# A one-core decoder block: square-root seeds in the first and last norm, and a re-timed attention loop

## The chip, the cores and the metric

The kernel runs on one core of a Trainium2 chip. The metric is the device time of one execution in microseconds. Before the change, three runs took 1623.13 to 1624.22 us, with a median of 1623.73 us. One further execution was taken with the hardware profiler, and all views of the profile come from it. The engines are named as the profile names them: PE is the matrix engine (PEld its weight loads), DVE the vector engine, ACT the activation engine, POOL the general engine, SP the queue that issues most transfers. A `q` behind an engine's name means its sequencer.

## The reference

The program computes one layer of a decoder on 512 positions of width 1024, in float32:

```python
h = layer_norm(x, ln_in_g, ln_in_b)
mix = hybrid_mixer(h, ...)          # 16 SSD heads and 8 latent-attention heads, one output projection
h = layer_norm(DEEPNORM_ALPHA * h + mix, ln_mix_g, ln_mix_b)
ffn = peer(h, w_query, sub_keys, u_table, v_table)   # 8 heads, top 16 of 128 x 128 experts
h = layer_norm(DEEPNORM_ALPHA * h + ffn, ln_ffn_g, ln_ffn_b)

def layer_norm(x, g, b):
    mu = jnp.mean(x, -1, keepdims=True)
    var = jnp.mean(jnp.square(x - mu), -1, keepdims=True)
    return (x - mu) * lax.rsqrt(var + NORM_EPS) * g + b
```

The attention of one head is a causal softmax of scores (a part without and a part with rotary positions) times values, for four blocks of 128 queries. The SSD branch is a chunked state-space recurrence, gated with silu(z) and scaled by a root-mean-square norm; then both branches go through one output projection of 2048 x 1024.

## The kernel before

All instructions are written in one order by hand (`tc.manual_schedule()`); each engine and each queue runs its own in that order, and semaphores hold an instruction until what it reads is there and what it overwrites has been read. Every product is made of three (`mm3`, L72 to L74): weights and activations are each split into a high part in a shorter format and a low part, the remainder.

**Weights.** `Stream` (`win`) carries all weights. Per item there is a load (L91, on SP, into `wir`, three buffers), a high part by ACT (`his`, L109, into `wih`) and a low part by DVE (`splits`, L119, into `wil`). `get(n)` (through `item()`) first splits the items up to n + `la`, and a split issues the load of the item three further on. `la` is 2 before the attention.

**First norm** (L265 to L286). x lies in `XH` in four blocks of 128 positions and is worked in two pairs. For a pair, DVE makes the statistics (L268, L269), then the inverse root of the variance by `rsqrt` (L133 to L138: a seed from the exponent's bits and three Newton rounds), then `nm` (L274). ACT and DVE scale the blocks (L279, L281), and PE transposes them into eight PSUM banks (L284). Behind the first pair ACT makes the high parts of weights 0 and 1 (`win.his(2)`). Then, for each of eight slices, ACT and DVE write `ht`, `HH` and `HL` (L291 to L296), and PE starts the first two projections with them (L72 to L74).

**Attention** (the loop over `st` from 0 to 38, L832 on). Step `st` belongs to head `st // 4` and query block `st % 4`, and the stages of a head follow one another as a pipeline. In the order of the code a step holds: `p_scale` of the block two steps back (reciprocal of the sum on DVE, L783; scaling on ACT for the two longer blocks, L785, on DVE for the two shorter, L787); `p_tr` of six steps back (transposes of the weights, L796, whose high part ACT and whose low part DVE writes, `evac`, L695 and L696); `scores` (into PSUM, maximum on DVE, L769); `y_tr` in eight of the steps (`GST[3]` is 7, so steps 16 to 23: transposes of the SSD result, L541, read out by ACT and DVE, L547 and L548); one part of the projections of the next head (`q_pe` with L708 and L711, `qk_nope`, `v_proj`; each first part takes one item of weights); from step 28 one weight of the output projection for the fourth block of positions (`w_out_step`); `p_exp` (ACT, L777); in steps 8 to 15 one part of the SSD norm (`gate2`, L521 to L534); and `p_v`, the product with the values of seven steps back, whose result `MO` goes through `evac` into `MH` and `ML`. `p_tr`, `scores` and `y_tr` share one ring of four PSUM buffers (`pt`); the projections and the values of `v_proj` share two (`pu`). After the loop comes the tenth weight for the fourth block, and then the output projection for the other three blocks, with its own items.

**After that** come the second norm, the PEER stage (queries, top 16, and two long passes over the tables, with gathers for the fourth block), in which PE is busy nearly without a gap, and the last norm. `ln_out(b)` (L1504 to L1528) does it for blocks 0, 1 and 2 in turn: add the residual, statistics, the inverse root by `norm_chain` (L144 to L154, the same bit seed and three rounds), two scalings, and the transfer to the output. For block 2 the two first scalings (L1518) stand between the Newton operations.

## Time and profile before

| what | value |
|---|---|
| median of three runs | 1623.73 us (1623.13 to 1624.22) |
| profiled execution | 1623.08 us |
| its span, first to last instruction | 1621.3 us |
| PE / DVE / ACT / POOL busy | 1581.0 / 1357.4 / 708.1 / 481.4 us |
| mean granted clock of PE | 0.998 |
| HBM traffic | 360 MB read, 32 MB written |

The time holds the span and what the execution needs around it. Lines of the page's groups name the source line, engine, operation, and out<-in by the program's names; behind the bar stand busy time and the mean duration of one in ns. In the order of time a line begins with its start and its duration in us, and a bracket at its end tells how long the engine sat idle and what ended that. In PE's lines the durations of neighbours overlap, since products are pipelined; what counts is the distance of the starts.

### The profile page before, as it was taken

The page shows a single profiled execution, that of the slowest core. Times are in us where ns is not written, and L with a number is a line of the kernel's source. Part 1 is how long each engine was busy: PE and PEld are TensorE (multiplying, and loading weights), DVE is VectorE, ACT ScalarE, POOL GpSimd, SP SyncE. Part 2 cuts the span into 40 slices and gives each one's busy share as a digit, 9 for nine tenths or more (in the row PEclk, how much of TensorE's full clock was granted, in tenths as well). Part 3 has the DMA queues.
Part 4 walks back from the last instruction along what each step waited for, and adds up shares of the span by engine and source line. Part 5 has one row for each costly group of instructions (what it writes and reads, how often), then busy time and mean ns, then how long its engine had stood idle before and what let it go on. Part 6 is the DMA issues. An engine that isn't in the chain of part 4 may idle for free.

```text
span 1621.3 us, 23808 instructions
## 1 busy us (share of the span) xinstructions
PE 1581.0 (98%) x8643; PEld 1393.0 (86%) x8643; DVE 1357.4 (84%) x2564; ACT 708.1 (44%) x1231; POOL 481.4 (30%) x340
## 2 busy tenths in 40 slices
PE   6999999999999999999999999999999999999997
PEld 5777878888888999999999999999999999888886
DVE  8978667747799999998478888888888888889877
ACT  5575467641433445555433433333333333333341
POOL 0000010000133223100035555555555555555300
PEclk9999999999999999999999999999999999999999
DMA  6242122364432459767689999999999999999973
GB/s 243 94 157 91 46 77 57 114 235 143 133 92 81 136 179 344 272 241 255 201 282 360 358 341 342 359 352 343 349 351 350 343 343 360 353 338 362 334 226 118
DMA packets 152253, 395.42 MB, mean 244 GB/s; under 512 B 12776, under 2 KB 65720, under 8 KB 150344
## 3 DMA queue, kind: packets, MB, share of 16 engines
q1 hardware_dynamic: 108408, 238.35, 43.3%
q0 software_dynamic: 43584, 155.29, 26.1%
q8 instruction: 68, 1.11, 0.3%
q14 instruction: 49, 0.40, 0.1%
q10 hardware_dynamic: 144, 0.26, 0.0%
HBM read 359.99 MB, written 31.78 MB: 242 GB/s over the span
## 4 chain that ended last, share of the span: by engine, by line
PE 74%; DVE 18%; ACT 3%; issue 3%; DMA 2%; SPq 0%; DVEq 0%; ACTq 0%
PE va L1377 10%; PE va L1381 10%; PE va L1378 10%; PE pu L72 9%; PE pu L74 8%; PE pu L73 8%; PE pa L74 3%; PE pa L73 3%; PE pa L72 3%; DVE ij L1134 2%; DVE wil L119 2%; DVE t L955 1%; DMA wir<-ut 1%; DVE ti L959 1%; DVE ti L952 1%
## 5 line engine op out<-in xcount | busy, mean ns | idle before, releaser
L109 ACT ACTIVATE wih<-wir 128x1024 fp32r<-128x1024 f32 (+2 forms) x269 | 278.0, 1034 | 275.0 <-DMA wir<-v 94.4
L119 DVE TENSOR_TENSOR wil<-wir,wih 128x1024 fp32r<-128x1024 f32 (+1 forms) x254 | 301.9, 1189 | 98.7 <-ACT wih L109 53.8
L74 PE MATMUL pu<-XTH,wil 128*128 128x368 f32 x1008 | 331.8, 329 | 1.0 <-DVE wil L119 0.9
L72 PE MATMUL pu<-XTH,wih 128*128 128x368 f32 x904 | 299.0, 331 | 1.3 <-ACT act L1230 1.3
L73 PE MATMUL pu<-XTL,wih 128*128 128x368 f32 x904 | 296.9, 328 | 0.0
L1378 PE MATMUL va<-wil,Ph 128*128 128x512 f32 x726 | 282.7, 389 | 0.0
L1415 POOL DMA_INDIRECT row<-u,ix x128 | 190.9, 1491 | 256.7 <-DVE row L1426 126.1
L1415 POOL DMA_INDIRECT row<-v,ix x128 | 193.8, 1514 | 168.5 <-DVE ac L1432 142.9
L74 PEld LDWEIGHTS pu<-XTH,wil 128*128 128x128 f32 x1008 | 189.1, 188 | 1.7 <-DVE wil L119 1.6
L72 PEld LDWEIGHTS pu<-XTH,wih 128*128 128x128 f32 x904 | 169.5, 188 | 4.8 <-ACT act L1230 1.9
L73 PEld LDWEIGHTS pu<-XTL,wih 128*128 128x128 f32 x904 | 169.8, 188 | 2.9
L1377 PE MATMUL va<-wih,Ph 128*128 128x512 f32 x432 | 168.6, 390 | 0.0
L1432 DVE SCALAR_TENSOR_TENSOR ac<-row,hd,ac 128x1024 f32<-128x1024 f32 x128 | 164.0, 1281 | 3.5 <-DMA row<-v,ix 1.2
L1378 PEld LDWEIGHTS va<-wil,Ph 128*128 128x128 f32 x726 | 136.3, 188 | 25.8
L1230 ACT ACTIVATE act<-pu 128x368 f32<-128x368 f32 x126 | 59.9, 476 | 219.5 <-PE pu L74 219.4
L1426 DVE SCALAR_TENSOR_TENSOR row<-row,x 128x1024 f32<-128x1024 f32 x128 | 150.3, 1219 | 3.9 <-DMA row<-u,ix 3.7
L109 ACT ACTIVATE wihx<-wir 128x1024 fp32r<-128x1024 f32 x67 | 71.1, 1061 | 146.1 <-DMA wir<-v 120.5
L1381 PE MATMUL va<-wih,Pl 128*128 128x512 f32 x432 | 133.3, 390 | 0.0
L119 DVE TENSOR_TENSOR wil<-wir,wihx 128x1024 fp32r<-128x1024 f32 x62 | 75.8, 1223 | 51.4 <-issue 36.8
L1377 PE MATMUL va<-wihx,Ph 128*128 128x512 f32 x294 | 114.9, 391 | 0.0
L1381 PEld LDWEIGHTS va<-wih,Pl 128*128 128x128 f32 x432 | 81.0, 188 | 17.2
L1377 PEld LDWEIGHTS va<-wih,Ph 128*128 128x128 f32 x432 | 81.2, 188 | 15.9
(458 smaller groups left out, 3066.3 us busy)
## 6 DMA issues: line engine op xcount, KB each, us to landing
wir<-ut SPq DMA_DIRECT2D x128, 512.0 KB, 5.7
wir<-v SPq DMA_DIRECT2D x128, 512.0 KB, 6.6
gsp<-stg SPq DMA_DIRECT2D x12, 1920.0 KB, 7.4
gt<-gsp SPq DMA_DIRECT2D x30, 768.0 KB, 9.9
wir<-wo SPq DMA_DIRECT2D x26, 512.0 KB, 3.6
wir<-wf SPq DMA_DIRECT2D x18, 512.0 KB, 3.3
wir<-wqr SPq DMA_DIRECT2D x16, 512.0 KB, 3.6
de<-acd POOLq DMA_DIRECT2D x8, 512.0 KB, 5.2
```

The costliest lines, as they stand in the source:

```text
L72: T.matmul(ps, lh, rh, start=start, stop=False)
L73: T.matmul(ps, lh, rl, start=False, stop=False)
L74: T.matmul(ps, ll, rh, start=False, stop=stop)
L109: A.activation(h, r, AF.Copy)
L119: self.lo(n).tensor_tensor(l, r, h, op=OP.subtract)
L1230: A.activation(ACT[c][:, :NU], ps, AF.Gelu)
L1377: T.matmul(va[b][e], Ph[:, bs], h[:, cs], start=c == 0, stop=False)
L1378: T.matmul(va[b][e], Ph[:, bs], l[:, cs], start=False, stop=False)
L1381: T.matmul(va[b][e], Pl[:, bs], h[:, cs], start=False, stop=c == 127)
L1415: G.indirect_dma_start(out=R[s], out_offset=None, in_=I["u"] if s < 128 else I["v"], in_offset=bass.IndirectOffsetOnAxis(ap=ix[:, s % 128: ...
L1426: V.scalar_tensor_tensor(r, r, 1.0, x3, op0=OP.mult, op1=OP.mult, accum_out=hd[:, s:s + 1])
L1432: V.scalar_tensor_tensor(ac, r, hd[:, s - 128:s - 127], ac, op0=OP.mult, op1=OP.add)
```

## The change

It touches three places.

1. First norm: `sqrt_rs` takes the place of `rsqrt`. ACT computes the square root of variance plus eps; DVE takes the reciprocal as the seed and makes one Newton round (square, product, correction). A tile `eps` is added, and a root of ones early on ACT. The high part of weight 0 is made behind the second pair's root, ahead of its scaling, and that of weight 1 behind the second pair's transposes.
2. Attention: `la` is 1 up to step 25, 2 from step 26, 1 at step 36 and 2 after the loop. `y_tr` moves from steps 16 to 23 into steps 17 to 24. For the last head (h = 7) all four blocks are scaled on DVE.
3. Last norm: block 2 uses `sqrt_chain`, in which ACT makes the root and DVE the reciprocal and one round; the two first scalings of the block stand ahead of the reciprocal and ahead of the round. Ahead of the last products, ACT runs a `Square` and a `Sqrt` on one column.

```diff
+    def sqrt_rs(p, v, shape, tag, eps):
+        h, q, y, a = (p.tile(shape, F32, name=tag + n) for n in "hqya")
+        A.activation(q, v, AF.Sqrt, bias=eps)
+        V.tensor_scalar(h, v, EPS, -0.5, op0=OP.add, op1=OP.mult)
+        V.reciprocal(y, q)
+        V.tensor_tensor(a, y, y, op=OP.mult)
+        V.tensor_tensor(a, a, h, op=OP.mult)
+        V.scalar_tensor_tensor(y, a, 1.5, y, op0=OP.add, op1=OP.mult)
+        return y
+
+    def sqrt_chain(p, mv, tag, out, eps):
+        h, q, a, y = (p.tile([128, 1], F32, name=tag + n) for n in "hqay")
+        A.activation(q, mv[:, 1:2], AF.Sqrt, bias=eps)
+        V.tensor_scalar(h, mv[:, 1:2], EPS, -0.5, op0=OP.add, op1=OP.mult)
+        yield
+        V.reciprocal(y, q)
+        yield
+        V.scalar_tensor_tensor(a, y, h, y, op0=OP.mult, op1=OP.mult)
+        yield
+        V.scalar_tensor_tensor(y, a, 1.5, y, op0=OP.add, op1=OP.mult)
+        out.append(y)
+        yield
...
+    eps = lnp.tile([128, 1], F32, name="eps")
+    V.memset(eps, EPS)
+    w0 = lnp.tile([128, 1], F32, name="w0")
+    A.activation(w0, ones[:, 0:1], AF.Sqrt, bias=eps)
...
-        ve = lnp.tile([128, 2], F32, name="ve", bufs=2)
-        V.tensor_scalar(ve, mv4[:, bs, 1], EPS, None, op0=OP.add)
-        rs = rsqrt(lnp, ve, [128, 2], "l0")
+        rs = sqrt_rs(lnp, mv4[:, bs, 1], [128, 2], f"l{p}", eps)
         V.scalar_tensor_tensor(nm, mv4[:, bs, 0], -1.0, rs, op0=OP.mult, op1=OP.mult)
+        if p:
+            win.his(1)
...
-        if p == 0:
-            win.his(2)
+    win.his(2)
     win.splits(1)
...
-        if qb > 1:
+        if qb > 1 and h < 7:
             A.activation(P[:, :n], P[:, :n], AF.Copy, scale=sm)
...
+    win.la = 1
     for st in range(39):
         h, q = divmod(st, 4)
+        if st == 26:
+            win.la = 2
...
-        if GST[3] + 9 <= st < GST[3] + 17:
-            y_tr(st - GST[3] - 9)
+        if GST[3] + 10 <= st < GST[3] + 18:
+            y_tr(st - GST[3] - 10)
...
             if st < 37:
+                win.la = 1 if st == 36 else 2
                 w_out_step(acc3, (3,), st - 28)
...
+    win.la = 2
     w_out_step(acc3, (3,), 9)
...
-        ch = norm_chain(fin, mv, "lf", o)
+        ch = sqrt_chain(fin, mv, "ls", o, epf) if b == 2 else norm_chain(fin, mv, "lf", o)
         for i, _ in enumerate(ch):
             yield
-            if b == 2 and i in (2, 4):
-                cs = ce[i // 2 - 1]
+            if b == 2 and i in (0, 1):
+                cs = ce[i]
...
+    w0 = fin.tile([128, 1], F32, name="w0")
+    epf = fin.tile([128, 1], F32, name="epf")
+    V.memset(epf, EPS)
+    A.activation(w0, xr[2][:, 0:1], AF.Square)
+    A.activation(w0, w0, AF.Sqrt, bias=epf)
```

## The prediction

> **What bounds the kernel now.** I read the page first (busy shares, then the chain of work that ended last), then the busy time by stage, then PE's waits inside the attention, and last the order of time at the three places that the change touches.

> ```profile
> PE 1581.0 (98%) x8643; PEld 1393.0 (86%) x8643; DVE 1357.4 (84%) x2564; ACT 708.1 (44%) x1231; POOL 481.4 (30%) x340
> ...
> PE 74%; DVE 18%; ACT 3%; issue 3%; DMA 2%; SPq 0%; DVEq 0%; ACTq 0%
> ```
> ```profile
> 345.00:1594.00 1249.00, 1239.92 (x6904) 1115.34 (x6903) 1064.75 (x1989) 503.58 (x831) 465.88 (x307) 1.00 0.80 282
> 1594.00:1622.00 28.00, 17.43 (x77) 14.08 (x76) 21.68 (x57) 0.00 (x0) 0.00 (x0) 0.86 0.15 57
> ```
> The second view's columns are stretch, length, then busy time of PE, PE's weight loads, DVE, ACT and POOL. From 345 to 1594 us PE stands still for only 9 us in 1249. The order on every engine is written out, so whatever time the front half gains or loses moves this whole block and reaches the end. In the last 28 us PE stops early and DVE is busy for 21.7: the tail belongs to DVE. So three places count: when PE's first projection starts, what PE waits for in the attention, and the DVE chain of the tail. This is PE's wait list between 210 and 345 us (in total, times, longest):

> ```profile
> PE pt L541 <- DVE thl L696: 1.8, 1, 1.8
> PE pt L796 <- ACT P L785: 1.4, 2, 0.9
> PE po L73 <- DVE pt L696: 0.9, 1, 0.9
> ```
> These are the first SSD transpose (y_tr(0), step 16, 1.8 and, shown below, 0.45 more), the transposes that wait for scaled attention weights (0.9 of the 1.4 at step 34), and the last value product (step 38). The change aims at all three, so at most about 4 us are to be had in the attention.

> **Part 1, the first norm.**

> ```profile
> 7.10 0.17 DVE L272 TENSOR_SCALAR ve<-mv 128x2 f32<-128x2 f32 x1
> ...
> 9.66 2.37 ACT L279 ACTIVATE XH<-XH,nm,l0y 128x1024 f32<-128x1024 f32 x2 [4.19 <-DVE nm L274]
> ...
> 11.94 1.99 ACT L109 ACTIVATE wih<-wir 128x1024 fp32r<-128x1024 f32 x2
> ...
> 12.09 1.75 PE L284 MATMUL pa<-ident,XH 128*128 128x128 f32 x7 [0.66 <-ACT XH L279]
> ...
> 12.49 0.17 DVE L272 TENSOR_SCALAR ve<-mv 128x2 f32<-128x2 f32 x1
> ...
> 13.64 1.92 PE L284 MATMUL pb<-ident,XH 128*128 128x128 f32 x8
> ...
> 14.87 0.16 DVE L274 SCALAR_TENSOR_TENSOR nm<-mv,l0y 128x2 f32<-128x2 f32 x1
> ...
> 15.06 1.27 DVE L281 TENSOR_SCALAR XH<-XH,l0y,nm 128x1024 f32<-128x1024 f32 x2
> ...
> 16.66 1.45 ACT L291 ACTIVATE ht<-pa,PAR 128x512 f32<-128x512 f32 x2 [0.78 <-PE pa L284]
> 17.12 1.04 PE L284 MATMUL pb<-ident,XH 128*128 128x128 f32 x8
> ...
> 18.68 0.50 PE L73 MATMUL pa<-HL,wih 128*128 128x512 f32 x1 [0.22 <-DVE HL L296]
> ```
> ```profile
> L405 ACT ACTIVATE nA<-HR x1: 199/199/199, 56.2 to 56.2; 128x16 f32<-128x16 f32 x1
> ```
> Before, the seed, the three Newton rounds and nm take from 7.10 to 9.62 (ACT starts behind them at 9.66), and again from 12.49 to 15.03: 13 dependent operations, about 0.195 each from start to start. After: a square root on ACT, for which the small 0.199 activation is the nearest row (I take 0.22), then reciprocal, square, product, correction and nm, five operations at 0.195; h runs on DVE beside the root. That is 0.22 + 5 x 0.195 = 1.2 with the hand-over against 2.5, so 1.3 per pair of blocks. The second pair starts when the first's nm is done, so both add up: the second nm ends at about 12.5 instead of 15.03. The added memset and the root on constants lie in the time in which both engines wait for x.

> Not all of the 2.5 arrives. ACT's order changes too: before, both weight copies (1.99) filled its wait for the second nm; now one does and the second (1.0) comes after the half block of XH. With XH at 12.55 to 13.8 (DVE's 1.27), ACT runs copy (to 12.55), half block (to 13.36), copy (to 14.3), so ht can start at 14.3, where it was 16.66. PE is the next to be late. Its first pair's transposes wait for XH of the second block, which comes 1.3 earlier; 15 of them at about 0.22 (7 from 12.09 to 13.64) then run from 10.75 to about 14.0, and the second pair queues behind. There the pace matters: the last 8 took 1.04, half the time, so PE doubled its speed in between, at about 16.4. If the doubling comes as much earlier as the first work, 1.3, the second pair ends near 16.7, and the low-part product now at 18.68 runs at 16.8 (its HL ready at 16.5): 1.9 gained. If the doubling stays away until 17.6 the transposes end at 17.4 and 1.2 is left; if it does not matter, 2.3. I take 1.9 and keep 1.2 to 2.3. Loads are no obstacle to this: the second weight tile is only copied later than before.

> [...]

> **Part 2, the attention.** Steps st 0 to 38; before, weights are split two items ahead.

> ```profile
> 261.44 0.23 PE L766 MATMUL pt<-nub,idb 128*128 128x128 bf16 x1
> ...
> 264.13 0.69 ACT L777 ACTIVATE P<-pt,mx 128x512 f32<-128x512 f32 x1 [1.96 <-DVE mx L769]
> ...
> 264.49 0.33 PE L541 MATMUL pt<-ident,xs 128*128 128x128 f32 x1 [0.45 <-DVE xs L534]
> ...
> 266.32 0.42 DVE L696 TENSOR_TENSOR thl<-pt,thh 128x256 fp32r<-128x256 f32 x1 [1.83 <-ACT thh L695]
> ...
> 267.27 0.27 PE L796 MATMUL pt<-ident,P 128*128 128x128 f32 x1
> ...
> 294.37 0.69 ACT L777 ACTIVATE P<-pt,mx 128x512 f32<-128x512 f32 x1 [1.34 <-DVE mx L769]
> ...
> 294.44 0.23 PE L766 MATMUL pt<-nub,idb 128*128 128x128 bf16 x1
> ```
> (a) y_tr one step later. The waits of 1.8 + 0.45 at step 16 vanish, and PE runs on from the end of its scores (261.5) into the projection and value products, which took 2.7 behind y_tr (264.57 to 267.27); so it reaches step 17 at 264.2. What is late next is the PSUM ring of four that attention weights, scores and y_tr share: scores(4,1) needs the buffer of the exponent that ends at 264.8 (PE is there at 264.3: 0.5), and y_tr(0) then needs the one whose reader ends at 266.74 (PE there 0.9 later, at 265.7: 1.05). So 2.25 - 0.5 - 1.05 = 0.7 is won, not 2.25. At the far end y_tr(7) now falls into step 24, where it needs the buffer of the exponent that ends at 295.06, while PE's scores of that step (the 294.44 row is their last) are through at 294.47: 0.6 lost. Sum -0.1; bounds -2.0 (the ring catches up) and +1.0. The moved evacuations (one on ACT, one on DVE, 0.7 each) are the same eight; no DMA and no queue entry belongs to them.

> (b) Split one ahead. Up to step 25 each fetch splits the next item in place of the one after: the same number and nearly the same widths on ACT and DVE; the first fetch splits nothing, in a stretch where both idle: 0 (+-0.3). SP's loads follow one item later, with several steps of lead. The missing split is repaid at step 26, where two 1024-wide ones stand in a row.

> ```profile
> 305.60 0.55 DVE L696 TENSOR_TENSOR thl<-pt,thh 128x384 fp32r<-128x384 f32 x1
> ...
> 306.88 0.36 PE L72 MATMUL pt<-knh,qnh 128*128 128x256 f32 x1
> ...
> 331.38 1.23 DVE L119 TENSOR_TENSOR wil<-wir,wih 128x1024 fp32r<-128x1024 f32 x1 [0.43 <-ACT wih L109]
> ...
> 333.40 0.60 ACT L695 ACTIVATE MH<-po 128x512 fp32r<-128x512 f32 x1 [1.89 <-PE po L74]
> ...
> 333.89 1.05 ACT L109 ACTIVATE wih<-wir 128x1024 fp32r<-128x1024 f32 x1
> ```
> That puts 1.05 on ACT and 1.23 on DVE ahead of the low part at 305.60, which frees the buffer for the scores at 306.88. It would end at about 307.05 rather than 306.15, so +0.25 (0 to 1.2).

> (c) Scaling of the last head on DVE.

> ```profile
> 323.60 0.72 ACT L785 ACTIVATE P<-P,sm 128x512 f32<-128x512 f32 x1 [1.43 <-DVE sm L783]
> ...
> L534 DVE TENSOR_SCALAR xs<-xs,rqy x4: 477/479/481, 251.3 to 264.0; 128x512 f32<-128x512 f32 x4
> ```
> 0.72 on ACT becomes 0.48 on DVE (the scale of the gates, same shape and operation), without the hand-over. At step 32 ACT is rid of its scaling, so the weight copy and DVE's split behind it run about 0.9 earlier, and the last scaling ends at about 323.1 instead of 324.3. PE's wait of 0.88, with the pipeline fill 1.1, goes: -1.1 (bounds -0.4, DVE's shorter operation alone, and -1.3).

> (d) One ahead at step 36. The split at 331.38 stood before the last low part that PE waited 0.91 for; it goes, and some 0.3 of that wait stays, as the hand-over ACT, DVE, PE. But its item is the first of the next output projection. It is now split after the last head's evacuation: MH (0.60), copy (1.05), difference (1.23), about 3.05 us after the last value product, while PE has only the 6 products of the tenth weight (1.4) and one more to fill that time. PE waits about 1.5 in its place, most of it before that weight's low half. In sum +0.25 (bounds -0.9, if the copy is early enough, and +1.5).

> The attention together: -0.1 + 0.25 - 1.1 + 0.25 = -0.7.

> **Part 3, the last norm.**

> ```profile
> 1613.20 0.21 DVE L1510 BATCH_NORM_AGGREGATE fmv<-fst 128x2 f32<-128x12 f32 x1
> ...
> 1613.89 0.74 DVE L1518 SCALAR_TENSOR_TENSOR xr<-xr,fmv,R 128x512 f32<-128x512 f32 x1
> 1614.55 0.22 DVE L152 SCALAR_TENSOR_TENSOR lfa<-lfy,lfh 128x1 f32<-128x1 f32 x1
> ...
> 1616.43 1.41 DVE L1527 SCALAR_TENSOR_TENSOR xr<-xr,lfy,R 128x512 f32<-128x512 f32 x2
> ```
> Now the two big operations come straight after h: the first at 1613.52, reciprocal 0.66 later, the second 0.07 after that, the two corrections at 1614.9 and 1615.15, and the last scaling at 1615.35 instead of 1616.43: -1.1. The root (some 0.25 on an idle ACT from 1613.45) is covered by the first big operation (0.74). The table load that the new root needs falls at about 1592.5, when ACT has finished; the last output descriptor leaves ACT after 1617. Bounds -0.9 and -1.2.

> **Sum.** -1.9 - 0.7 - 1.1 = -3.7. The profiled execution took 1623.08 (span 1621.3 and 1.8 around it); that makes 1619.4. The median of the runs is 1623.73, 0.65 more, so 1620.0.

> **Rivals.**
> 1. The waits simply go: nothing else is late at steps 16, 24, 26 and 38. Then 2.2 + 1.1 + 0.9 in the attention with 1.9 + 1.1: 1616.5. For it: ACT and DVE have idle time at each place. Against: the 264.13 and 266.32 rows are late through ACT and DVE alone, and the change does not move them.
> 2. The attention turns sour within its bounds (+0.6, +0.7, -0.6, +0.6: +1.3 in place of -0.7): 1622.0, no change that can be told. What speaks for it is that rings and double splits cost twice where ACT and DVE alternate.
> 3. The start does not do what it says: the root and Identity/Copy sit in different tables and ACT reloads between them.

> ```profile
> L456 ACT ACT_TABLE_LOAD x3 | 3.8, 1283 | 0.0
> ```
> Each reload is 1.28, one after the first root, two around the second, and some 2 of them land on the path: 1622. Against: all 18 reloads of the trace stand at exponents, Silu, Gelu or the very first activation; none before a Copy or Square. [...]
> 4. Slower: one ahead is too little. The place is q_pe to qk_nope (steps 4, 12, 20), where the item is now split one step before its use, and every later fetch.

> ```profile
> 223.99 0.83 DVE L119 TENSOR_TENSOR wil<-wir,wih 128x640 fp32r<-128x640 f32 x1 [1.73 <-ACT wih L109]
> ...
> 225.06 0.79 PE L72 MATMUL pu<-qlh,wih 128*128 128x512 f32 x1
> ```
> The split in that slot ends at 224.82, PE begins there at 225.06 and reads the low half two products later: a slack of 0.2 to 0.9. It takes 7 us of lateness, 0.6 at each of some 12 fetches, to end 3.25 above before: 1627.

> **How the numbers follow.** About 0.2% (3.25 us) is what a measurement here can tell from no change, so "faster" is below 1620.5. Forecast 0.52 (its own 1618.5 to 1621.5, of which 0.37 lies below 1620.5), rival 1 0.2, rival 2 0.18, rival 3 0.05, rival 4 0.05. So faster 0.57, same 0.38, slower 0.05. The range runs from half-way to rival 1 to just past rival 2: 1617.2 to 1622.5.

> **What would show it.** The first norm: nm at 8.3 and 12.5, the low-part product at 16.4 to 17.5, one table load before 5 us and none until Silu. Attention: no wait of y_tr at step 16 but waits of PE on buffers at steps 17 and 24; no PE wait on scaled weights in the last head; a PE wait on the first item of the output projection of 1 us or more. Tail: last scaling 2.2 after the aggregate instead of 3.2. The prediction is wrong if a table load stands inside the first 15 us, if PE's waits between 345 and 1594 grow with the shift, or if the wait at the output projection is absent.

## The result and the profile after

The changed kernel takes 1620.57 us (median of 13 executions, 1619.77 to 1621.46); the kernel before took 1624.22 beside it on the same chip (13, 1622.49 to 1627.75). The ratio is 0.9977, 95% interval 0.9968 to 0.9985: faster by 3.65 us, or 0.23%. The profiled execution took 1619.77 with a span of 1617.9. Source lines above 140 have moved: L299 is the old L274 (`nm`), L306/L308 the scaling of x, L567 is `y_tr`, L721/L722 is `evac`, L811/L813 is the scaling of the weights, L822 is `p_tr`.

The page of the changed kernel, busy shares and the chain that ended last, and its busy time by stage:

```profile
PE 1582.2 (98%) x8643; PEld 1393.5 (86%) x8643; DVE 1355.1 (84%) x2548; ACT 709.9 (44%) x1236; POOL 475.5 (29%) x340
...
PE 76%; DVE 16%; ACT 3%; issue 3%; DMA 1%; DVEq 0%; ACTq 0%
```
```profile
345.00:1594.00 1249.00, 1240.70 (x6908) 1116.13 (x6907) 1066.03 (x1992) 505.18 (x834) 459.74 (x307) 1.00 0.80 282
1594.00:1622.00 28.00, 15.14 (x67) 12.20 (x65) 19.39 (x50) 0.30 (x1) 0.00 (x0) 0.87 0.15 57
```

The shares hardly move, and PE's idle time between 345 and 1594 us has not grown (8.3 us, before 9.1). What counts is where the shift of PE's order of time arises. The table below gives the start of the same instruction in three traces, the third that of an experiment below (weights split two ahead throughout); in brackets the distance to before:

| instruction | before | after | two ahead throughout |
|---|---|---|---|
| low-part product of the first projection | 18.68 | 16.85 (-1.83) | 17.00 (-1.68) |
| mask product (last of the scores), step 7 | 231.88 | 230.00 (-1.88) | 230.01 (-1.87) |
| the same, step 10 | 241.70 | 240.08 (-1.62) | 239.79 (-1.91) |
| step 16 | 261.44 | 259.98 (-1.46) | 259.60 (-1.84) |
| step 18 | 271.56 | 269.11 (-2.45) | 268.54 (-3.02) |
| step 25 | 297.88 | 296.57 (-1.31) | 295.83 (-2.05) |
| step 31 | 316.82 | 315.56 (-1.26) | 314.78 (-2.04) |
| last `p_tr` | 330.81 | 328.86 (-1.95) | 327.67 (-3.14) |
| first low part of the output projection of three blocks | 334.79 | 333.22 (-1.57) | 331.30 (-3.49) |
| first transposes after the second norm | 397.43 | 396.00 (-1.43) | 393.96 (-3.47) |
| 65th product behind the top-16 search | 611.00 | 608.76 (-2.24) | 607.45 (-3.55) |
| last value product of the PEER stage | 1611.04 | 1608.76 (-2.28) | 1607.38 (-3.66) |
| span | 1621.33 | 1617.87 (-3.46) | 1616.50 (-4.83) |

So the first norm wins 1.83 to 1.88, the attention gives back 0.45 (from -1.88 at step 7 to -1.43), 0.8 comes between 397 and 609 us, where no line of code has changed, and the tail wins the last 1.2 (from -2.28 to -3.46).

The first norm of the changed kernel in order of time (start, duration, engine, line, operation, in brackets the idle time before and what ended it):

```profile
7.17 0.29 ACT L143 ACTIVATE l0q<-mv,eps 128x2 f32<-128x2 f32 x1 [4.83 <-DVE mv L296]
...
8.28 0.16 DVE L299 SCALAR_TENSOR_TENSOR nm<-mv,l0y 128x2 f32<-128x2 f32 x1
...
12.43 0.16 DVE L299 SCALAR_TENSOR_TENSOR nm<-mv,l1y 128x2 f32<-128x2 f32 x1
...
14.83 1.45 ACT L317 ACTIVATE ht<-pa,PAR 128x512 f32<-128x512 f32 x2 [0.44 <-PE pa L311]
...
15.64 1.04 PE L311 MATMUL pb<-ident,XH 128*128 128x128 f32 x8
...
16.85 0.50 PE L73 MATMUL pa<-HL,wih 128*128 128x512 f32 x1
```

`nm` stands at 8.28 and 12.43, the product at 16.85. The root takes 0.29, not the 0.22 assumed; `h` is computed on DVE beside it.

PE's waits of the changed kernel between 210 and 345 us (in total, times, longest), and some of them in order of time:

```profile
PE pt L567 <- DVE thl L722: 0.9, 1, 0.9
PE px L73 <- DVE wil L119: 0.8, 1, 0.8
PE pt L72 <- ACT P L803: 0.7, 2, 0.5
PE pt L822 <- ACT P L811: 0.7, 1, 0.7
...
PE pt L822 <- DVE P L813: 0.2, 1, 0.2
```
```profile
263.50 0.39 PE L72 MATMUL pt<-knh,qnh 128*128 128x256 f32 x1 [0.51 <-ACT P L803]
265.35 0.66 PE L567 MATMUL pt<-ident,xs 128*128 128x128 f32 x4 [0.92 <-DVE thl L722]
...
331.96 0.49 PE L72 MATMUL px<-wih,zt 128*128 128x512 f32 x1 [0.25 <-ACT wih L109]
333.22 0.50 PE L73 MATMUL px<-wil,zt 128*128 128x512 f32 x1 [0.77 <-DVE wil L119]
```

The 1.8 of the first `y_tr` has gone and 0.51 and 0.92 stand at step 17, as forecast. The last head waits 0.2 for its scaling. The last value product no longer waits 0.91, but the first item of the output projection waits 0.25 and 0.77. The wait for a scaling by ACT at step 10, 0.53 before, has grown to 0.68.

The tail:

```profile
1589.86 1.28 ACT L1566 ACT_TABLE_LOAD   x1 [0.23 <-DVE epf L1564]
...
1610.92 0.21 DVE L1541 BATCH_NORM_AGGREGATE fmv<-fst 128x2 f32<-128x12 f32 x1
...
1613.06 1.42 DVE L1558 SCALAR_TENSOR_TENSOR xr<-xr,lsy,R 128x512 f32<-128x512 f32 x2
```

The last scaling starts 2.14 after the aggregate, where it was 3.23.

### The profile page after: what moved, and what is told of

Read it like the earlier page. It is cut to its first block, busy times and chain, and to the rows that moved or that the text cites. A ratio compares the mean times of both kernels' runs of the same rounds, so it can differ in the third digit from the quotient of the medians.

```text
span 1617.9 us, 23797 instructions
## 1 busy us (share of the span) xinstructions
PE 1582.2 (98%) x8643; PEld 1393.5 (86%) x8643; DVE 1355.1 (84%) x2548; ACT 709.9 (44%) x1236; POOL 475.5 (29%) x340
## 4 chain that ended last, share of the span: by engine, by line
PE 76%; DVE 16%; ACT 3%; issue 3%; DMA 1%; DVEq 0%; ACTq 0%
PE va L1408 10%; PE va L1412 10%; PE va L1409 10%; PE pu L72 9%; PE pu L74 9%; PE pu L73 9%; PE pa L72 3%; PE pa L74 3%; PE pa L73 3%; DVE ij L1165 2%; DVE wil L119 2%; DVE t L986 1%; PE pw L73 1%; PE pw L74 1%; PE pw L72 1%
## 5 line engine op out<-in xcount | busy, mean ns | idle before, releaser
L109 ACT ACTIVATE wih<-wir 128x1024 fp32r<-128x1024 f32 (+2 forms) x269 | 278.0, 1035 | 300.6 <-DMA wir<-ut 99.8
L119 DVE TENSOR_TENSOR wil<-wir,wih 128x1024 fp32r<-128x1024 f32 (+1 forms) x254 | 301.9, 1190 | 101.6 <-ACT wih L109 56.7
L74 PE MATMUL pu<-XTH,wil 128*128 128x368 f32 x1008 | 331.7, 329 | 1.0 <-DVE wil L119 0.9
L72 PE MATMUL pu<-XTH,wih 128*128 128x368 f32 x904 | 299.0, 331 | 1.0 <-ACT act L1261 1.0
L73 PE MATMUL pu<-XTL,wih 128*128 128x368 f32 x904 | 296.8, 328 | 0.0
L1446 POOL DMA_INDIRECT row<-v,ix x128 | 186.6, 1457 | 175.8 <-DVE ac L1463 150.8
L74 PEld LDWEIGHTS pu<-XTH,wil 128*128 128x128 f32 x1008 | 189.0, 187 | 1.7 <-DVE wil L119 1.6
L72 PEld LDWEIGHTS pu<-XTH,wih 128*128 128x128 f32 x904 | 169.7, 188 | 4.3 <-ACT act L1261 1.3
L73 PEld LDWEIGHTS pu<-XTL,wih 128*128 128x128 f32 x904 | 169.7, 188 | 2.9
L109 ACT ACTIVATE wihx<-wir 128x1024 fp32r<-128x1024 f32 x67 | 71.1, 1061 | 150.0 <-DMA wir<-v 129.4
L119 DVE TENSOR_TENSOR wil<-wir,wihx 128x1024 fp32r<-128x1024 f32 x62 | 75.8, 1223 | 43.5 <-issue 32.1
L1412 PEld LDWEIGHTS va<-wih,Pl 128*128 128x128 f32 x432 | 81.1, 188 | 17.2
```

The source lines that it names most:

```text
L72: T.matmul(ps, lh, rh, start=start, stop=False)
L73: T.matmul(ps, lh, rl, start=False, stop=False)
L74: T.matmul(ps, ll, rh, start=False, stop=stop)
L109: A.activation(h, r, AF.Copy)
L119: self.lo(n).tensor_tensor(l, r, h, op=OP.subtract)
L1412: T.matmul(va[b][e], Pl[:, bs], h[:, cs], start=False, stop=c == 127)
```

## The experiments

The same instruction varies between executions: in the seven profiled kernels that have the new first norm and nothing more ahead of the attention, the low-part product starts between 16.65 and 17.52, the mask product of step 7 between 229.80 and 230.17. So shifts below are taken between two instructions of the same trace where that matters. All ratios are to the kernel before on the same chip.

**The kernel before, once more** (no edit), to see what repeats.

> The kernel before, unchanged, profiled a second time. If PE's waits between 575 and 611 us vary from run to run, they differ here from the first profile's (0.93, 0.23, 0.81 us); the waits of the attention (1.8, 0.45, 0.88, 0.91) are set by the order and are the same within 0.1. If those waits are fixed too, the extra 0.8 us of the changed kernel is an effect of the change.

It took 1623.42. Every row of the table up to 397 us lies 0.05 to 0.20 ahead of the first profile, the 65th product behind the top-16 search 0.24 behind it. The waits of the attention repeat to 0.02; the stretch from 397 to 609 us does not: it took 213.57 there and 213.86 here. PE's waits show where such differences come from. Below are waits of before (first group), of the last-norm kernel further down, which has the code of before in this stretch (second group), and of the changed kernel:

```profile
PE pw L1157 <- DVE g L1139: 0.8, 1, 0.8
...
DVE gT L1123 <- ACT gT L1122: 0.8, 1, 0.8
ACT wihx L109 <- DMA wir<-ut: 0.6, 1, 0.6
```
```profile
PE pw L1180 <- DVE g L1162: 2.0, 1, 2.0
ACT wihx L109 <- DMA wir<-ut: 1.8, 1, 1.8
DVE gT L1146 <- ACT gT L1145: 1.8, 1, 1.8
```
```profile
PE pw L1188 <- DVE g L1170: 0.3, 1, 0.3
```

Where one weight lands late (`wir<-ut`), ACT copies it late (`wihx`) and reads out the transposed result of the top-16 search behind it late (`gT`); DVE waits for that, and PE for the table `g` that DVE builds from it. In the changed kernel the copy does not wait at all.

**The three places one by one**, each the kernel before with that part of the change alone.

The first norm:

```diff
-        rs = rsqrt(lnp, ve, [128, 2], "l0")
+        rs = sqrt_rs(lnp, mv4[:, bs, 1], [128, 2], f"l{p}", eps)
...
+        if p:
+            win.his(1)
...
-        if p == 0:
-            win.his(2)
+    win.his(2)
```

> The kernel before with the first norm alone changed. By my sum the low-part product of the first projection starts at 16.8 to 16.9 us (before 18.68), the attention's scores and the output projection lie 1.84 earlier with the same waits of PE in between (1.8 at step 16, 0.9 at step 34, 0.9 at step 38), and the time is 1.8 us less. In the changed kernel PE gained another 0.8 us between 575 and 611 us, which no part of the change explains. If that comes from the earlier start, this kernel's distance grows from 1.84 to 2.6 there; if it is a variation from run to run, it stays 1.84 or goes either way.

Median 1622.66 (1621.34 to 1625.33), ratio 0.9989 (0.9980 to 0.9999). The low-part product starts at 17.11, the mask product of step 7 at 229.85 (-2.03). But 1.3 of that is lost at once at step 17 and another 2.6 near 600 us, so that this profile ends 1.8 later than that of before. The cause of the first, and of part of the second, is treated below.

The attention:

```diff
-        if qb > 1:
+        if qb > 1 and h < 7:
...
+    win.la = 1
...
+        if st == 26:
+            win.la = 2
...
-        if GST[3] + 9 <= st < GST[3] + 17:
-            y_tr(st - GST[3] - 9)
+        if GST[3] + 10 <= st < GST[3] + 18:
+            y_tr(st - GST[3] - 10)
...
+                win.la = 1 if st == 36 else 2
```

> The kernel before with the attention's edits alone. The changed kernel's trace has the attention 0.47 us longer than before (1.90 ahead at its start, 1.43 at its end). By that the output projection of this kernel starts 0.4 to 0.5 us later than before and the time is the same within 0.1%. The rival, that the attention's edits gained and something else lost, has it 0.7 us earlier, as I forecast.

Median 1623.64 (1622.95 to 1627.96), ratio 1.000 (0.999 to 1.001). From step 7 to the transposes after the second norm it goes from -0.18 to +0.32: the attention by itself costs 0.5 in the trace. It was said to win 0.7.

The last norm:

```diff
-        ch = norm_chain(fin, mv, "lf", o)
+        ch = sqrt_chain(fin, mv, "ls", o, epf) if b == 2 else norm_chain(fin, mv, "lf", o)
...
-            if b == 2 and i in (2, 4):
-                cs = ce[i // 2 - 1]
+            if b == 2 and i in (0, 1):
+                cs = ce[i]
```

> The kernel before with the last norm alone changed. PE's work lies where it was; from the last block's statistics to the last scaling it takes 2.15 instead of 3.2 us, and the time is 1.1 us less. The rival, that the table load or the root gets in the way of the last output, has no gain or less than half of it.

Median 1623.40 (1621.67 to 1627.93), ratio 0.9994 (0.9985 to 1.0004). From the last value product (+3.95) to the end of the span (+2.79) it wins 1.16, as in the full change. The +3.95 comes from two places in front, at step 17 (+1.3) and near 600 us, though up to there this kernel has the code of before.

**How far ahead weights are split.** First two ahead at step 36 alone, then throughout:

```diff
-                win.la = 1 if st == 36 else 2
+                win.la = 2
```

> The changed kernel, but weights two ahead at step 36 again (only there). By my step (d) the first item of the output projection is then ready in time: PE's waits of 0.25 and 0.77 in front of it go, about 0.35 of wait comes back at the last value product, and the second product of that projection starts at about 332.3 instead of 333.2: 0.9 us less than the changed kernel. The rival, that the split delays the last low part as it did before the change (0.9 wait), has it even.

Median 1620.29 (1619.78 to 1622.88), ratio 0.9975 (0.9965 to 0.9986). From step 31 (+0.20 to after) to the first low part of the output projection (-0.27) it wins 0.47: this is what one ahead costs at step 36.

```diff
-    win.la = 1
     for st in range(39):
...
-        if st == 26:
-            win.la = 2
...
-                win.la = 1 if st == 36 else 2
```

> The changed kernel with weights two ahead throughout. If one ahead only moves work (my steps b and d), PE's waits at steps 8 and 10 fall back from 0.17 and 0.68 to 0.02 and 0.53 us, the wait at the output projection goes, and the attention ends about 1.2 us earlier than in the changed kernel. If one ahead relieves ACT and DVE, it ends later, by 0.5 us or more.

Median 1618.48 (1618.15 to 1620.58), ratio 0.9966 (0.9953 to 0.9978). PE's order of time in this kernel around the same two places, and below it two pairs of rows, the first of each pair from the changed kernel, the second from this one:

```profile
329.34 0.39 PE L73 MATMUL po<-pt,vh 128*128 128x256 f32 x1 [0.65 <-DVE pt L722]
...
331.07 0.39 PE L72 MATMUL px<-wih,zt 128*128 128x512 f32 x1
331.30 0.40 PE L73 MATMUL px<-wil,zt 128*128 128x512 f32 x1
```
```profile
226.57 0.83 DVE L119 TENSOR_TENSOR wil<-wir,wih 128x640 fp32r<-128x640 f32 x1
...
239.03 0.33 PE L822 MATMUL pt<-ident,P 128*128 128x128 f32 x1 [0.68 <-ACT P L811]
```
```profile
226.56 0.68 DVE L119 TENSOR_TENSOR wil<-wir,wih 128x512 fp32r<-128x512 f32 x1
...
238.75 0.33 PE L822 MATMUL pt<-ident,P 128*128 128x128 f32 x1 [0.53 <-ACT P L811]
```

The wait of 0.65 for the last value product is back and the 1.02 at the output projection is gone. Earlier, at the same moment (226.6) DVE splits 512 columns here and 640 in the changed kernel: the same items, but each falls into the slot of another. DVE's rows are 0.15 later behind this split and 0.28 later behind the next one (512 columns at 236.13 where 384 stand here at 235.98), and so are ACT's scaling of step 10 and PE behind it: its start is 0.28 later. The table shows the sum: the two kernels are level at step 7; from there two ahead wins 0.3 by step 10, 0.74 by step 25, 0.78 by step 31, 0.4 more by the last `p_tr` and 0.7 more at the output projection: 1.9 in all, of which 0.47 belongs to step 36 and some 1.45 to the rest (1.49, from step 7 on, between this kernel and the one with two ahead at step 36 alone). Its median lies 2.1 below that of after, though from another chip, and the intervals of the two ratios overlap; the rows are the firmer evidence.

**The last head scaled on ACT**, the rest as after:

```diff
-        if qb > 1 and h < 7:
+        if qb > 1:
```

> The changed kernel with the last head's two longer blocks scaled on ACT again. The trace of the change shows 0.69 us gained there, so PE's wait on the scaled weights at step 34 grows from 0.19 to about 0.88 and the attention ends 0.7 us later. If ACT's time there is hidden behind the splits, it ends within 0.2 us of the changed kernel.

Median 1621.97 (1621.38 to 1622.50), ratio 0.9984 (0.9975 to 0.9994). PE waits for it in the last head:

```profile
PE pt L822 <- ACT P L811: 1.5, 1, 1.5
```

From step 31 (-0.15 to after) to the last `p_tr` (+1.20) it loses 1.35. The wait was 0.88 before; it is 1.53 here, because ACT is late. Counted from the last mask product (step 31), its last scaling starts 6.78 later in before and 7.43 later here, and those 0.65 are what the wait has grown by. The lateness arises at step 26, where two copies of 1024 columns stand in a row on ACT (2.01) and two splits on DVE (2.35 in the changed kernel). The DVE scaling is worth 1.1 with weights two ahead (the table's third column, -2.04 to -3.14) and 1.35 with one ahead, where it also covers lateness that one ahead has made.

**`y_tr` at its old step**, the rest as after:

```diff
-        if GST[3] + 10 <= st < GST[3] + 18:
-            y_tr(st - GST[3] - 10)
+        if GST[3] + 9 <= st < GST[3] + 17:
+            y_tr(st - GST[3] - 9)
```

> The changed kernel with the SSD transposes back at steps 16 to 23. My step (a), the ring that they share is late either way, says no difference: waits of 2.2 at step 16 for 0.5 + 0.9 at step 17 and 0.33 at step 24, in sum within 0.3 us at the end of the attention. That the move removes a wait of its own says 1.5 to 2.2 us longer.

Median 1622.06 (1620.68 to 1624.44), ratio 0.9984 (0.9975 to 0.9994): 1.5 above after, where the waits alone say 0.1. The two medians come from different chips, and the intervals of the ratios overlap; in the traces the distance to after goes from -0.03 at step 16 to +1.17 at step 25. PE's order of time, and the busy time by stretch (stretch, length, busy time of PE, its weight loads, DVE, ACT and POOL, then the granted clock of PE):

```profile
262.01 0.80 PE L567 MATMUL pt<-ident,xs 128*128 128x128 f32 x3 [1.83 <-DVE thl L722]
...
263.71 0.63 PE L73 MATMUL pu<-qll,wih 128*128 128x512 f32 x1
264.13 0.63 PE L74 MATMUL pu<-qlh,wil 128*128 128x512 f32 x1
```
```profile
258.75:262.17 3.42, 1.59 (x11) 1.10 (x10) 2.48 (x7) 1.94 (x5) 0.00 (x0) 1.00 0.31 73
262.17:265.58 3.41, 3.22 (x10) 2.33 (x10) 1.58 (x6) 2.93 (x7) 0.00 (x0) 0.50 0.02 5
```

Behind the wait the products start 0.42 to 0.43 apart (263.71 to 265.41), where the same products of the changed kernel start 0.23 apart (260.34 to 261.96) at a granted clock of 1.00; here it is 0.50 for 3.41 us. That costs 1.2 (from step 16 to 18 PE takes 11.29, before 10.12). The profiles of the first-norm and the last-norm kernels, with `y_tr` at its old step too, show the same, and once more near 600 us, where PE waits 2 us for `g`; in the other twelve profiles that wait is 0.1 to 1.3, and nothing is halved there. The first-norm kernel:

```profile
258.61:262.02 3.41, 1.59 (x12) 1.08 (x10) 2.47 (x7) 1.53 (x4) 0.00 (x0) 1.00 0.21 38
262.03:265.44 3.41, 2.98 (x8) 2.40 (x9) 1.59 (x5) 3.15 (x7) 0.00 (x0) 0.50 0.02 5
593.12:596.53 3.41, 1.17 (x20) 1.09 (x20) 3.27 (x4) 1.56 (x3) 0.00 (x0) 1.00 0.66 191
596.53:599.94 3.41, 3.41 (x23) 3.41 (x22) 3.38 (x3) 2.24 (x4) 0.00 (x0) 0.50 0.29 117
```

The two profiles of the kernel before have the wait of 1.8 and 0.45 as well, and no drop. There the change of the clock to full at the start (16.51 us in the first profile) lies so that the boundary of two such stretches falls into the wait:

```profile
258.86:262.27 3.41, 2.81 (x17) 2.04 (x15) 2.51 (x6) 2.48 (x6) 0.00 (x0) 1.00 0.69 187
262.27:265.68 3.41, 1.74 (x9) 1.34 (x10) 2.19 (x7) 1.55 (x4) 0.00 (x0) 1.00 0.02 5
265.68:269.09 3.41, 3.41 (x23) 3.02 (x22) 2.47 (x6) 2.64 (x8) 0.00 (x0) 1.00 0.00 0
```

Theory, worked out from these rows: a stretch of 3.41 us in which PE stands still for more than about half (1.83 in the 258.75 row of the kernel with `y_tr` put back, against 1.67 in the 262.27 row of before) is followed by one at half speed. It is tried by **filling the wait**: `y_tr` at the old step, with 26 small products ahead of it that add zeros to a sum of step 16.

```diff
+        if st == 16:
+            for _ in range(26):
+                T.matmul(MO[2][:, 0:128], idb, zb, start=False, stop=False)
         if GST[3] + 9 <= st < GST[3] + 17:
```

> The changed kernel with the SSD transposes back at steps 16 to 23, as in the run on that move alone, and with 26 small products that add zeros to the open value sum put into TensorE's stream at step 16, ahead of the first transpose: TensorE works through most of its 2.2 us there. Theory: what the old place costs beyond its wait is the halved clock that follows a TensorE pause of about 2 us. Then the granted clock stays at 1.00 from 262 to 266 us in the profile, the wait before the first transpose falls below 0.8, the time from there to step 24 is that of the changed kernel within 0.4, and the median is 1620.3 to 1621.0 against 1622.06 without the filling. Rival: the halving has nothing to do with the pause (heat, a power rule, the kind of work). Then 3.41 us at half speed still appear near 262 in about every second execution and the median stays at 1621.8 to 1622.5, or above by what the filling adds.

Median 1620.78 (1619.94 to 1625.70), ratio 0.9984 (0.9975 to 0.9992). By stretch:

```profile
260.70:264.12 3.42, 2.61 (x24) 2.02 (x21) 2.12 (x7) 1.63 (x4) 0.00 (x0) 1.00 0.00 0
264.12:267.53 3.41, 3.41 (x22) 2.98 (x22) 2.60 (x6) 2.62 (x8) 0.00 (x0) 1.00 0.00 0
```

The clock stays full, and the mask product of step 25 lies where it lies after (-0.17, as at the steps before 16). By its ratio this kernel is level with the one before it, since before had 1623.79 beside this one and 1624.65 beside that one. But the executions of before with a mean clock above 0.997 have nearly the same median on both chips (1623.31 and 1623.22), and measured from these the filling wins: 1620.78 against 1622.06.

The mean granted clock of each execution points the same way without a profile, though roughly. In the profiles it is 0.998 or 0.999 without a halved stretch, and one such stretch takes some 0.001 off (half of 3.41 in 1620 us), so 0.998 may hide one. It is 0.997 or less in 51 of 81 executions of the kernel before that ran beside the experiments, in 8 of 10 with the first norm alone, 7 of 10 with the last norm alone and 5 of 10 with `y_tr` put back; with the filling in 1 of 12. With `y_tr` one step later it is none of 13 after, of 8 with two ahead at step 36 and of 10 with ACT scaling, 2 of 10 with the attention alone, and 1 of 6 with two ahead throughout. By chip, the executions of before with the lower clock have medians of 1624.7 to 1625.1, the others of 1623.2 to 1623.6; their share differs by chip too (9 of 22 beside the filling, 16 of 21 beside `y_tr` put back).

**The price of a reload.** An activation of another table set behind the first pair's root; its result is used by nothing.

```diff
+        if not p:
+            A.activation(w0, ones[:, 0:1], AF.Silu)
```

> The changed kernel with one activation of another table set on a constant (128x1, its result is used by nothing) between the first pair's root and its scaling, so that ACT loads a table for it and another one for the second root. It prices the third rival of the prediction. If a reload costs the 1.28 of the load row, the first scaling of x starts 1.28 plus 0.3 minus what lies beside the correction on VectorE (1.0) later, some 0.5 to 0.7, the second root comes 1.3 later, and the low-part product goes from 16.85 to 18.0 to 18.7 us: two reloads give back the better part of the 1.84 that the first norm won. [...] If the loads are hidden, it stays within 0.3 of 16.85.

ACT of this kernel:

```profile
7.33 1.28 ACT L300 ACT_TABLE_LOAD   x1
8.62 0.20 ACT L300 ACTIVATE w<-ones 128x1 f32<-128x1 f32 x1
...
11.11 1.28 ACT L143 ACT_TABLE_LOAD   x1
12.40 0.30 ACT L143 ACTIVATE l1q<-mv,eps 128x2 f32<-128x2 f32 x1
```

Two loads of 1.28 with the next activation 0.01 behind each. The low-part product comes at 17.39, 0.54 later than after: below what was expected, since DVE's correction covers most of the first load (the scaling starts 0.25 later); the second makes ACT's scaling of the second pair 1.1 later, of which PE's transposes cover a part. How much is not settled by this one execution: PE's clock came up at 14.49 us in it and at 15.39 in after. Of the 0.54, 0.23 are left at 397 us. It took 1621.52; the other 1.4 by which its span exceeds after's arise behind 397 us, where its code is the same.

**PE at work before x arrives**, on top of two ahead throughout: products of a constant into a bank that the transposes overwrite, 44 and then 28.

```diff
+    for _ in range(44):
+        T.matmul(PS8[7][:, 0:128], ones, ones, start=True, stop=True)
     for p in range(2):
```

> The version with weights split two ahead throughout (1618.48), with 44 products of a constant tile on TensorE from 1 us on, into a bank that the transposes overwrite, while x is being loaded. Theory: the transposes of the first norm run at half pace (0.22 each up to 15.4 us, 0.13 after) because the clock comes up only after some us of work; work done before 9.8 us brings it up earlier. Then the first pair's 15 transposes end 1.3 us earlier, the second pair's are set by XH (13.9) and end at about 15.2 instead of 16.7, HL follows the first of them, and the low-part product moves from 17.00 to 15.9 to 16.5: 0.5 to 1.1 gained, median 1617.4 to 1618.0. Rival 1: ACT's chain behind XH (copy 1.04, then ht 1.45) sets the product, and the pace does not matter: within 0.2 of 17.00 and 1618.5. Rival 2: the early products delay the first transpose beyond 9.9, and the start becomes later: above 17.2.

Median 1620.96 (1618.77 to 1622.70), ratio 0.9979 (0.9970 to 0.9989). The products ran until 12.51, the first transpose came 2.4 late, and the low-part product still came 0.46 earlier than without them (16.54), as the transposes took 1.04 for each eight, where without them the second, third and last eight took 1.91, 1.92 and 1.12. Then 0.9 are lost at 780 us, where PE waits 1.81 for ACT in place of 0.92, and 0.8 between 1240 and 1300 us (0.45 of it a wait for a weight's low part), and 4 of 10 executions have a clock of 0.997 or less.

> Weights split two ahead throughout, with 28 early products of a constant in place of 44. The 44 ran as 88 passes of 0.13 to 12.51 us, so that the first transpose came 2.4 us late (12.35 for 9.91), yet the low-part product 0.46 earlier (16.54 for 17.00), but the median rose from 1618.48 to 1620.96. 56 passes end at about 8.4 us, ahead of the first XH. Theory A, the start alone counts and the rest of that rise was the overrun or chance: the transposes go at 0.13 from 9.9 on, the low-part product comes at 15.9 to 16.5, the median at 1617.3 to 1618.2. Theory B, the early work only shifts when the clock's fixed windows fall and when later transfers and waits meet, which costs more than it wins: the product comes at the same 15.9 to 16.5, the median at 1619.3 to 1621.5 and the granted clock of many executions is 0.997 as with the 44. Theory C: TensorE's pause between 8.4 and 9.9 halves the clock again and the product stays at 16.8 to 17.2.

Median 1618.09 (1617.74 to 1619.55), ratio 0.9959 (0.9946 to 0.9973). PE:

```profile
1.07 8.02 PE L291 MATMUL pb<-ones 128*128 128x128 f32 x56 [1.07 <-DVE eps L285]
...
13.42 1.09 PE L313 MATMUL pa<-ident,XH 128*128 128x128 f32 x8 [0.73 <-DVE XH L310]
...
16.22 0.50 PE L73 MATMUL pa<-HL,wih 128*128 128x512 f32 x1 [0.22 <-DVE HL L324]
```

The product stands at 16.22, 0.78 ahead, and the scores lie some 0.7 ahead; now PE waits for XH. The clock is 0.997 in 1 of 5 executions. By the end 0.2 of it is left in this profile. This is the lowest median of the study, though it can't be told from the 1618.48 without the early products.

## Why the prediction was right in its sum and wrong in a step

Forecast 1620.0, measured 1620.57. The time is well inside the range, but that the sum is so close is partly luck: a step that lost more than forecast was made up for by terms that the forecast did not have.

- **Part 1, -1.9: right.** -1.83 at the product and -1.88 at step 7, `nm` at 8.3 and 12.4 as said. The root was 0.07 longer than assumed. That the product came at just -1.83 is a draw: it goes with the clock's first rise, 15.39 us in this execution and 16.51 in that of before, and over the seven kernels with this first norm the product goes from 16.65 (rise at 14.95) to 17.52 (rise at 16.95). By step 7 they lie 1.71 to 2.07 ahead of before. The profile's record of the clock begins with that rise; ahead of it seven transposes of before take 1.55 (12.09 to 13.64), behind it eight take 0.83 (17.12 to 17.95). No run shows the 17.6 up to which the lower bound let the doubling stay away: in the profiles without early products the first rise comes between 14.5 and 17.3 us. That the pace of the transposes matters, which the bounds 1.2 to 2.3 rested on, is shown by the run with 28 early products: with the first rise at 4.3 us at the latest, the low-part product came a further 0.78 earlier.
- **(a) `y_tr` later, -0.1: right as to the waits, wrong as to their worth.** The two waits at step 17 were forecast as 0.5 and 1.05 and are 0.51 and 0.92; the one at step 24, forecast as 0.6, is 0.33. From step 16 to 25 the shift changes by +0.15 after, and by -0.21 with two ahead. But the step costed waits alone. In three of the five profiles with `y_tr` at its old step and the pause not filled, the clock behind the pause was 0.50 for 3.41 us: put back, `y_tr` costs 1.2 in the trace (1.5 in the median), and with the pause filled nothing in the trace (0.2 in the median). That is the part of the result that no step foresaw.
- **(b) one ahead, +0.25: the step that failed.** It measures some 1.45. The prediction said that up to step 25 the cost is 0 because each fetch splits "the same number and nearly the same widths". The widths are those of other items: 640 columns stand where 512 stood and 512 where 384 stood, and at step 10 ACT and DVE have no slack for it. 0.74 has arisen by step 25, where 0 (+-0.3) was forecast. At step 26, where the forecast put its +0.25, PE loses next to nothing (0.78 by step 31), but ACT and DVE fall 0.65 behind, and PE pays for that in the last head and behind it, the remaining 0.7. Which slots besides step 10 make up the 0.74 was not followed row by row.
- **(c) the last head on DVE, -1.1: right with two ahead (1.1).** In the changed kernel it takes away 1.35, part of which (b) had put there.
- **(d) one ahead at step 36, +0.25: right in kind, too small.** The wait of 0.91 at the last value product has gone, and the first item of the output projection waits 1.02 in place of the estimated 1.5; the net is +0.47.
- **The attention, -0.7, is +0.45 in the trace.** Rival 2 (the attention turns sour, +1.3) was nearer to it than the forecast.
- **Part 3, -1.1: right.** 2.14 from the aggregate to the last scaling against 3.23.
- **What made up for it.** By the rows the parts sum to -1.88 + 0.45 - 1.1 = -2.5. The median fell by 3.65. Executions of before with a clock above 0.997 have medians of 1623.2 to 1623.6, some 2.8 above after's; the rest, about 0.9, is then the halving, which shows in 51 of 81 executions of before and in none of after's 13. That is an estimate, since the clocks of the 13 executions beside after are not on record. In the pair of profiles, neither of which is halved, the missing 0.8 lies between 397 and 609 us. That stretch takes 212.76 in the profile of after, 213.57 and 213.86 in the two of before, and 213.3 to 214.2 in those of the nine other kernels in which nothing is halved there: the profile of after has a short draw, and it is also the fastest of its 13 executions. PE's wait for `g` makes most of the difference (0.34 after, 0.81 and 1.07 in the two of before), and behind it stands the landing of one weight; why that varies stays open.
- **The other rivals.** 1 (the waits simply go, 1616.5) did not come: the ring of four buffers is late as said. 3 (table reloads): the change adds one load, at the root of the tail, and its first stands at 0.75 us in place of 4.19; two reloads cost 0.54 at the product and 0.23 at 397 us in the one profile that has them, where the rival put 2 for up to three. 4 (q_pe to qk_nope late at each fetch) did not come as described, but its idea, a small lateness at every fetch, is what (b) underrated.

## What to carry to other kernels

That the number of operations stays the same does not make a fetch free when it moves by one slot: write down which width lands in which slot, and look at the slots in which the helpers have no slack. Cost a wait of PE by more than its length: here, behind the wait of 1.8 us for the first `y_tr`, the work ran at a granted clock of 0.50 for 3.41 us in three of five profiles, so a single profile does not show what such a wait costs in the median. A change made of several parts can hit its total while one part loses; undoing one part at a time found some 1.9 us in the attention that the total hid.

## What the runs showed of the hardware

Why the kernel with 44 early products loses its 1.8 us behind 700 us stays open. Its profile shows no halving, and its idlest stretches there (1.53 at 690 us, 1.49 at 748 us) stand in the profile of after as well (1.52 and 1.50).
